# Layer 1's value products taken two steps in a row, first transfers in another order, last product in two pieces

## The chip, the cores and the metric
The kernel runs on one core of a Trainium2 chip. The metric is the device time of one execution in microseconds, as the median of several runs. The engines are named as in the profile: PE is TensorE (matrix products; PEld are its weight loads), DVE is VectorE, ACT is ScalarE, POOL is GpSimd, and SP (SyncE) issues the transfers (DMA). PSUM is the memory into which TensorE writes its products.

## The reference
Two layers run over 512 latent and 256 context tokens with D = 1024. Six modulation rows come from the conditioning vectors (adaLN). Layer 0 mixes tokens by windowed attention with 2 key/value heads and a sink, layer 1 by differential attention; behind each stands a squared-ReLU MLP of width 4096. Only the latent tokens are returned, so layer 1's context tokens serve as keys and values alone.
```python
mod_x = jax.nn.silu(c) @ w_ada[i] + b_ada[i]
hx = x * (1.0 + sc1) + sh1
# layer 1, in each of 8 heads
s = jnp.einsum('bqhtd,bkhtd->bhtqk', qblk, keys) * scale
p = jax.nn.softmax(s, axis=-1)
a = p[:, :, 0] - lam * p[:, :, 1]
o = jnp.einsum('bhqk,bkhe->bqhe', a, v_all)
o32 = o32 * lax.rsqrt(jnp.mean(jnp.square(o32), axis=-1, keepdims=True) + SUBLN_EPS)
# both layers
x = layer_norm(alpha * x + g1 * ax, ln1_g[i], ln1_b[i])
fx = sqrelu_mlp(x * (1.0 + sc2) + sh2, mlp_w1[i], mlp_w2[i])
x = layer_norm(alpha * x + g2 * fx, ln2_g[i], ln2_b[i])
```

## The kernel before
All data are fp32. A weight or activation is split into a high part that TensorE takes (fp32r) and the low rest, and a product is three matmuls (`mm3`, lines 322 to 324: high times high, then each low part times the other's high). `wsplit` loads a weight tile of 128x1024, ACT casts its high part (w_h, line 264), DVE subtracts to get the low part (w_l, line 312).

TensorE's order is written by a planner: `Flow` runs generators (projections, scores, attention, MLP) against a model of the engines' times and picks at each step who issues next; what it picks is fixed when the program is built. The other engines follow the order in which the generators emit. Output tiles in PSUM come from two sets of slots, 2 of 1024 columns for the scores (s_ps) and 4 of 512 columns for all else, so a tile can begin when the engine that reads the former one is done.

**Start.** `load_const` loads small constants, `dma` all larger tiles, all from SP's one queue. cT, badaT (bias of the modulation), ident (the identity for transposes) and lnT (layer norm parameters) are the first four; then `start_load(0)` issues four w_ada tiles, the first two tiles of the transposed x, the first key/value weight (a_wkv) and the first query weight. TensorE multiplies w_ada (ada_ps, line 364), ACT copies the rows (ada_rows), TensorE transposes them (ada_t, line 388, with ident), and DVE makes the modulation (mods) of them. hx = x times scale plus shift is then made by ACT (high part) and by DVE and POOL (low part), and the key/value products (kv_ps) follow, k-block by k-block. `setup` loads further constants later.

**Layer 1's attention** runs over 8 heads. `proj1` projects one 128-token block tb at a time (qkv_ps, 24 matmuls, issued in sixes; 384 columns for the four latent blocks, tb 0 to 3, and 256 for the two context blocks), `post1` makes rope (DVE, POOL), splits v (vt), k (sk) and q (sq), and transposes the last two (kT_ps line 1251, qT_ps line 1266). `scores1` forms the scores (s_ps, line 1347) for a 128-query block; DVE takes the negative maximum (nm), ACT the exponential, DVE the difference of the two maps (rc, nl, e). `att1` transposes e (pT_ps, line 1413), splits it (pT), and multiplies with v: one value step `av` is six matmuls of 128x256 into o_ps (line 1385). A head has six transposes and six value steps, and in each pass through its loop `att1` takes either a transpose (if `room()`) or one value step. After two heads each (0 and 1, 2 and 3, 4 and 5, 6 and 7) the norm over the head is made: rms_ps (line 1444), rmsT (1458), rr on POOL, rmsB (1473), rh and rl, rms_bc (1483, 1485), oraw. While this goes on the next head's context keys (sk, kT_ps) and projections run, and DVE splits the next head's weights (w_l of 768 columns).

**The end.** `tok_product` forms the second MLP product (y_ps, 512 columns, 24 matmuls for each token block and half). Behind the last one DVE multiplies by the gate (g_tmp, line 563), adds to acc, takes the statistics (bn), normalises, and SP sends acc out (line 1566).
```python
yield lambda: YES if room() or (pend and fl.ok(pend[0][3])) else NO
if room():
```


## Time and profile before

| what | value |
|---|---|
| median of 3 runs (lowest to highest) | 1686.93 us (1686.22 to 1688.71) |
| the profiled execution | 1690.51 us, span 1688.7 us, mean granted clock 0.991 |
| busy, share of the span | PE 96%, PEld 82%, DVE 57%, ACT 39%, POOL 20% |
| chain that ended last | PE 74%, DVE 10%, issue 5%, ACT 4%, DMA 3%, POOL 3% |

The profiled execution's time is the device time; the span is that from the first to the last instruction in its trace. Busy shares are means over the whole span. The chain is followed back from the last instruction to whatever released it each time. The granted clock is TensorE's, as a share of 2.4 GHz: 0.5 is 1.2 GHz. In rows of a timeline the first number is the start in us, the second the length; neighbouring rows of one group are merged (x4); in square brackets stands the idle time of the engine ahead of it and what ended it.

### The profile page before, as it was taken

To read this page: it belongs to the slowest core of one execution; us is meant where nothing else is said; L and a number is where in the kernel's file an instruction comes from. 1 tells how busy PE (TensorE), PEld (TensorE's weight loads), DVE (VectorE), ACT (ScalarE), POOL (GpSimd) and SP (SyncE) were. 2 spreads that over 40 slices of the span, in tenths; PEclk is the share of its full clock that TensorE was granted. 3 is DMA by queue.
4 is the path that set the end of the run, shared out by engine and by line. 5 is a ranking of instruction groups with operands and counts; after the bars stand their busy time and mean duration, and the time that the engine had idled before them with its cause. 6 is when DMAs were issued, how large, how long until landed. Compare 5 with 4: busy or idle time off the path is not lost.

```text
span 1688.7 us, 23443 instructions
## 1 busy us (share of the span) xinstructions
PE 1617.0 (96%) x9129; PEld 1392.0 (82%) x9129; DVE 956.7 (57%) x1811; ACT 658.2 (39%) x1281; POOL 344.4 (20%) x314
## 2 busy tenths in 40 slices
PE   6899999999999999999999999999989899999997
PEld 4787677789889889979978998999877788888886
DVE  3665787567756344344446777677656552332436
ACT  3454565362223113202316555555543533222230
POOL 1243544100001101243220223221101001103422
PEclk9999999999999999999999999999999899999999
DMA  9111451434445334234313122211133323132321
GB/s 365 42 51 37 170 175 35 136 125 130 145 138 162 100 125 150 100 113 139 109 59 110 51 69 67 69 45 38 47 113 111 102 80 120 63 125 75 112 88 50
DMA packets 57239, 174.77 MB, mean 103 GB/s; under 512 B 7144, under 2 KB 13096, under 8 KB 57128
## 3 DMA queue, kind: packets, MB, share of 16 engines
q1 hardware_dynamic: 57128, 173.27, 30.6%
q8 instruction: 72, 1.18, 0.3%
q14 instruction: 39, 0.32, 0.1%
HBM read 165.35 MB, written 7.90 MB: 103 GB/s over the span
## 4 chain that ended last, share of the span: by engine, by line
PE 74%; DVE 10%; issue 5%; ACT 4%; DMA 3%; POOL 3%; SPq 0%; POOLq 0%; DVEq 0%; ACTq 0%
PE y_ps L324 10%; PE y_ps L323 10%; PE y_ps L322 10%; PE h_ps L322 8%; PE h_ps L323 8%; PE h_ps L324 8%; PE o_ps L1031 2%; PE qkv_ps L322 2%; PE qkv_ps L323 2%; PE s_ps L1347 2%; PE qkv_ps L324 2%; DVE w_l L312 2%; PE pT_ps L1049 2%; DVE e L260 1%; PE o_ps L1385 1%
## 5 line engine op out<-in xcount | busy, mean ns | idle before, releaser
L264 ACT CAST w_h<-w_raw 128x1024 fp32r<-128x1024 f32 (+1 forms) x185 | 186.4, 1014 | 413.1 <-PE y_ps L324 208.6
L312 DVE TENSOR_TENSOR w_l<-w_raw,w_h 128x1024 fp32r<-128x1024 f32 (+1 forms) x185 | 220.9, 1205 | 220.6 <-ACT w_h L264 219.7
L323 PE MATMUL y_ps<-w_l,hid 128*128 128x512 f32 x640 | 252.9, 395 | 1.8 <-DVE w_l L312 1.7
L324 PE MATMUL y_ps<-w_h,hid 128*128 128x512 f32 x640 | 252.9, 395 | 0.7 <-DVE hid L260 0.7
L322 PE MATMUL y_ps<-w_h,hid 128*128 128x512 f32 x640 | 253.1, 395 | 0.0
L268 POOL TENSOR_TENSOR relu<-relu 128x768 f32<-128x768 f32 (+1 forms) x48 | 80.4, 1674 | 608.2 <-ACT relu L264 608.2
L324 PE MATMUL h_ps<-hx0m,w_l 128*128 128x384 f32 (+1 forms) x528 | 175.7, 333 | 1.6 <-DVE w_l L312 1.6
L322 PE MATMUL h_ps<-hx0m,w_h 128*128 128x384 f32 (+1 forms) x528 | 175.7, 333 | 0.2 <-ACT w_h L264 0.2
L323 PE MATMUL h_ps<-hx0m,w_h 128*128 128x384 f32 (+1 forms) x528 | 175.3, 332 | 0.0
L323 PEld LDWEIGHTS y_ps<-w_l,hid 128*128 128x128 f32 x640 | 120.4, 188 | 31.1 <-DVE w_l L312 3.3
L324 PEld LDWEIGHTS y_ps<-w_h,hid 128*128 128x128 f32 x640 | 120.4, 188 | 30.1 <-DVE hid L260 2.0
L322 PEld LDWEIGHTS y_ps<-w_h,hid 128*128 128x128 f32 x640 | 120.4, 188 | 28.7 <-ACT hid L264 0.4
L322 PE MATMUL qkv_ps<-w_h,hx 128*128 128x384 f32 (+1 forms) x384 | 127.8, 333 | 0.1
L323 PE MATMUL qkv_ps<-w_l,hx 128*128 128x384 f32 (+1 forms) x384 | 123.2, 321 | 0.3 <-DVE w_l L312 0.2
L324 PE MATMUL qkv_ps<-w_h,hx 128*128 128x384 f32 (+1 forms) x384 | 123.0, 320 | 0.0
L268 POOL TENSOR_TENSOR e<-e,sm 128x512 f32<-128x512 f32 (+2 forms) x96 | 94.1, 995 | 115.4 <-DVE sm L260 76.9
L322 PE MATMUL h_ps<-hx1m,w_h 128*128 128x512 f32 (+1 forms) x288 | 107.7, 374 | 3.6 <-ACT relu L264 3.6
L323 PE MATMUL h_ps<-hx1m,w_h 128*128 128x512 f32 (+1 forms) x288 | 107.3, 372 | 0.0
L324 PE MATMUL h_ps<-hx1m,w_l 128*128 128x512 f32 (+1 forms) x288 | 107.2, 372 | 0.0
L324 PEld LDWEIGHTS h_ps<-hx0m,w_l 128*128 128x128 f32 x528 | 99.1, 188 | 2.9 <-DVE w_l L312 2.9
L322 PEld LDWEIGHTS h_ps<-hx0m,w_h 128*128 128x128 f32 x528 | 99.1, 188 | 0.8 <-ACT w_h L264 0.6
L323 PEld LDWEIGHTS h_ps<-hx0m,w_h 128*128 128x128 f32 x528 | 99.1, 188 | 0.1
(225 smaller groups left out, 3112.6 us busy)
## 6 DMA issues: line engine op xcount, KB each, us to landing
w_raw<-in_w SPq DMA_DIRECT2D x128, 512.0 KB, 3.5
w_raw<-in_w_adaT SPq DMA_DIRECT2D x56, 512.0 KB, 3.5
w_raw<-in_w_ada SPq DMA_DIRECT2D x24, 512.0 KB, 4.0
w_raw<-in_b_w SPq DMA_DIRECT2D x32, 384.0 KB, 3.6
raw<-in_w_ada SPq DMA_DIRECT2D x16, 512.0 KB, 9.6
w_raw<-in_a_wq SPq DMA_DIRECT2D x8, 512.0 KB, 4.7
w_raw<-in_a_wo SPq DMA_DIRECT2D x8, 512.0 KB, 3.4
w_raw<-in_b_wo SPq DMA_DIRECT2D x8, 512.0 KB, 3.5
```

Of the source, the lines that this page charges most:

```text
L260: fn(**kw)
L264: fn(**kw)
L268: fn(**kw)
L312: last["split"] = nc.vector.tensor_tensor(**kw)
L322: nc.tensor.matmul(out=o, lhsT=lh, rhs=rh, start=start, stop=False)
L323: nc.tensor.matmul(out=o, lhsT=lh, rhs=rl, start=False, stop=False)
L324: last["pe"] = nc.tensor.matmul(out=o, lhsT=ll, rhs=rh, start=False, stop=stop)
L1031: nc.tensor.matmul(out=po[odd * HD:odd * HD + HD, 0:256], lhsT=vv[:, kb, kvh], rhs=pt_[:, odd * 256:odd * 256 + 256], start=(i == 0), stop ...
L1049: nc.tensor.transpose(out=pp[:, c * P:(c + 1) * P], in_=es[j][:, i * P:(i + 1) * P], identity=ident)
L1347: nc.tensor.matmul(out=sp[:, c * 512:c * 512 + 384], lhsT=qTt[:, tt, hl, qb * P:(qb + 1) * P], rhs=kS[:, tt, c * 384:c * 384 + 384], start ...
L1385: nc.tensor.matmul(out=po[:, qp * 256:(qp + 1) * 256], lhsT=vt[:, kb, vl], rhs=pt_[:, pl, a * 256:a * 256 + 256], start=(kp == 0 and pl == ...
```

## The change
Three places change. At the start badaT, ident and lnT leave the head of SP's queue: ident and badaT are issued after the first four w_ada tiles, lnT in `setup`, and a_wkv stands ahead of the two xT tiles. In `att1` a value step is taken only when two are ready (or the last ones, or when no pT buffer is free), and then both are issued in a row. In the last token block's last half of layer 1's MLP the product is formed in two pieces of 256 columns, each with its own g_tmp and add.
```diff
@@ -587,7 +587,7 @@
 
 
     def tok_product(pool, src, W, seq, acc, gates, done=None, st=None, scale=1.0, extra=None, pre={}, sink=None,
-                    late=(1,)):
+                    late=(1,), fine=False):
         st = st or {}
         Ws = {}
         if not callable(W):
@@ -601,6 +601,32 @@
                 yield sm_.ok
                 pt, u0 = psm("y_ps"), 0
                 give = lambda x, i=sm_.take(): sm_.give(i, x)
+            if fine and i == len(seq) - 1:
+
+                for c in range(2):
+                    if c:
+                        yield sm_.ok
+                        pt = psm("y_ps")
+                        give = lambda x, i=sm_.take(): sm_.give(i, x)
+                    cs_ = slice(half * 512 + c * 256, half * 512 + c * 256 + 256)
+                    tok = slice(tb * P, (tb + 1) * P)
+                    for u in range(4):
+                        w = Ws[half][u]
+                        yield w.t
+                        for k in (2 * u, 2 * u + 1):
+                            c_ = slice((k % 2) * 512 + c * 256, (k % 2) * 512 + c * 256 + 256)
+                            mm3(pt[:, 0:256], hxs(src, k, 0, tok), hxs(src, k, 1, tok), w.h[:, c_], w.l[:, c_], k == 0,
+                                k == KT - 1)
+                        p = fl.pe(6 * mm(256))
+                        if c:
+                            fl.finish(w.rel)
+                    tm = pool.tile([P, 256], F32, name="g_tmp", tag="tmp", bufs=2)
+                    m = dv(256, [p], nc.vector.tensor_tensor, out=tm, in0=pt[:, 0:256], in1=gates[0][:, cs_], op=ALU.mult)
+                    give(m)
+                    r = dv(256, [m], nc.vector.tensor_tensor, out=acc[tb][:, cs_], in0=acc[tb][:, cs_], in1=tm, op=ALU.add)
+                st[tb], r = stats(acc[tb], half, r, st.get(tb))
+                done(tb, st[tb], r)
+                continue
             left = {u for h, b in seq[i + 1:] if h == half for u in range(pre[(h, b)][2] if (h, b) in pre else 0, 4)}
             for u in range(u0, 4):
                 w = Ws[half][u]
@@ -730,13 +756,14 @@
                 gates = yield from row_gates()
             yield from tok_product(pool, hid, lambda half: [wsplit(t["w2"][l, ch, half, u]) for u in range(4)],
                                    [(h_, tb) for h_ in range(2) for tb in range(ntb)], acc, gates,
-                                   done if ch == 3 else None, extra=extra, sink=sum_up(ch, gates) if ch < 3 else None)
+                                   done if ch == 3 else None, extra=extra, sink=sum_up(ch, gates) if ch < 3 else None,
+                                   fine=l == 1 and ch == 3)
 
 
     l0 = ExitStack()
     apool = l0.enter_context(tc.tile_pool(name="apool0", bufs=4, reuse_waits="tile"))
     adap.append(l0.enter_context(tc.tile_pool(name="adap", bufs=1)))
-    badaT = load_const("badaT", [P, DEPTH, 6, KT], adap[0])
+    badaT = adap[0].tile([P, DEPTH, 6, KT], F32, name="c_badaT")
     hx = hx_tiles(apool, "hx0")
     st1 = {}
     y_spill = dram.tile([NTB, P, 512], F32, name="y_spill")
@@ -748,7 +775,6 @@
         cs = pool.tile([P, KT, 32], F32, name="cs", tag="cs")
         nc.vector.memset(cs, 0.0)
         nc.vector.tensor_copy(out=cs[:, :, 0:2], in_=sig)
-        nc.vector.tensor_copy(out=identr, in_=load_const("ident", [P, P], pool))
 
 
         def qtile(i, name, dt=F32R):
@@ -768,13 +794,15 @@
 
         def start_load(g):
             Wa = [ada_load(t["w_ada"][0, m, g, u], next(raws)) for m in (1, 0) for u in range(2)]
+            if g == 0:
+                nc.vector.tensor_copy(out=identr, in_=load_const("ident", [P, P], pool))
+                nc.sync.dma_start(out=badaT, in_=t["badaT"])
+                Wkv.append(wsplit(t["a_wkv"][0]))
             xs = []
             for k in (2 * g, 2 * g + 1):
                 x, gr, rr = next(raws)
                 x = x[:, 0:TOK]
                 xs.append((k, x, dma(TOK, [gr], out=x, in_=t["xT"][:, k]), rr))
-            if g == 0:
-                Wkv.append(wsplit(t["a_wkv"][0]))
             if g == 2:
                 hl = [pool.tile([P, 1024], F32R, name="w_kv", tag="x4", bufs=3) for _ in range(2)]
                 Wkv.append(wsplit(t["a_wkv"][1], hl=hl + [None, None]))
@@ -855,8 +883,9 @@
             nc.sync.dma_start(out=nsink, in_=t["a_sink"].broadcast_to([P, A_HEADS]))
             scale_inplace(nsink, -1.0)
             nc.sync.dma_start(out=mask, in_=t["mask"])
-
-        lnT = load_const("lnT", [P, DEPTH, 4, KT])
+            nc.sync.dma_start(out=lnT, in_=t["lnT"])
+
+        lnT = const.tile([P, DEPTH, 4, KT], F32, name="c_lnT")
         nsink = const.tile([P, A_HEADS], F32, name="nsink")
         mask = pool.tile([P, 6, P], F32, name="mask", tag="mask")
 
@@ -1397,8 +1426,11 @@
                 def room():
                     qp = i // 3
                     return i < 6 and len(ers) > qp * 2 + 1 and fl.ok([sm_.ok, xS1.ok, ers[qp * 2], ers[qp * 2 + 1]])
-                yield lambda: YES if room() or (pend and fl.ok(pend[0][3])) else NO
-                if room():
+
+                def ready_():
+                    return pend and (len(pend) > 1 or i == 6 or not fl.ok(xS1.ok)) and fl.ok([x[3] for x in pend[:2]])
+                yield lambda: YES if room() or ready_() else NO
+                if len(pend) < 2 and room() or not ready_():
                     if po is None:
                         yield sm_.spare
                         po = psm("o_ps")
@@ -1423,7 +1455,8 @@
                     pend.append((kp, qp, pt_, r, xi))
                     i += 1
                 else:
-                    p = av(*pend.pop(0))
+                    for _ in range(min(2, len(pend))):
+                        p = av(*pend.pop(0))
             st["att"] = hd_
 
 
```
**DVE at the start**, from the second group of mods to the first w_l (raw becomes x times scale plus shift, and from it hx's low part is made). Before:
```order
L260 TENSOR_TENSOR mods_81<-ada_red,c_badaT 128x4
L260 TENSOR_SCALAR raw_127<-raw_127,mods_81 128x512
L260 TENSOR_SCALAR raw_127<-raw_127,mods_81 128x256
L260 TENSOR_TENSOR hx_91<-raw_127,hx_91 128x512
L260 TENSOR_SCALAR raw_129<-raw_129,mods_81 128x512
L260 TENSOR_SCALAR raw_129<-raw_129,mods_81 128x256
L260 TENSOR_TENSOR hx_91<-raw_129,hx_91 128x512
L312 TENSOR_TENSOR w_l<-w_raw,w_h 128x1024 x2
```

After the change:
```order
L260 TENSOR_TENSOR mods_81<-ada_red,c_badaT 128x4
L312 TENSOR_TENSOR w_l<-w_raw,w_h 128x1024
L260 TENSOR_SCALAR raw_132<-raw_132,mods_81 128x512
L260 TENSOR_SCALAR raw_132<-raw_132,mods_81 128x256
L260 TENSOR_TENSOR hx_90<-raw_132,hx_90 128x512
L260 TENSOR_SCALAR raw_134<-raw_134,mods_81 128x512
L260 TENSOR_SCALAR raw_134<-raw_134,mods_81 128x256
L260 TENSOR_TENSOR hx_90<-raw_134,hx_90 128x512
L312 TENSOR_TENSOR w_l<-w_raw,w_h 128x1024
```

The first w_l (of a_wkv) now stands ahead of the six multiply-adds and subtractions, the second (of a_wq) stays behind them.

**PE at the passage from head 1 to head 2**, from rmsB to the first scores of head 2; of the qkv_ps matmuls of 128x384, which repeat in threes, one three is shown. Before, where twelve of them stand ahead of kT_ps and six behind it:
```order
L1473 MATMUL rmsB<-identr,rr 2x128 x4
L322 MATMUL qkv_ps<-w_h,hx_7757 128x384
L323 MATMUL qkv_ps<-w_l,hx_7757 128x384
L324 MATMUL qkv_ps<-w_h,hx_7757 128x384
L1251 MATMUL kT_ps<-identr,sk 128x128 x2
L1483 MATMUL rms_bc<-rh,id_8248 128x512
L1485 MATMUL rms_bc<-rl,id_8248 128x512
L1347 MATMUL s_ps<-kS_8975,qT_8976 128x384 x8
```

After the change, where six stand, behind kT_ps:
```order
L1506 MATMUL rmsB<-identr,rr 2x128 x4
L1280 MATMUL kT_ps<-identr,sk 128x128 x2
L322 MATMUL qkv_ps<-w_h,hx_7757 128x384
L323 MATMUL qkv_ps<-w_l,hx_7757 128x384
L324 MATMUL qkv_ps<-w_h,hx_7757 128x384
L1516 MATMUL rms_bc<-rh,id_8248 128x512
L1518 MATMUL rms_bc<-rl,id_8248 128x512
L1376 MATMUL s_ps<-kS_8975,qT_8976 128x384 x8
```

kT_ps (the last context block's keys) moved up to directly behind rmsB, past twelve projections. DVE's rows in this passage have a vt more ahead of three w_l and rl, which stand ahead of sk as before; after the change the passages from heads 1, 3 and 5 read alike on PE and DVE, as that from head 5 does before.

**PE in the middle of head 1**, from the last score tile to the projections behind it (the row of three qkv_ps is again shown once). Before, where 24 qkv_ps follow, six of tb 2 and 18 of tb 3:
```order
L1413 MATMUL pT_ps<-identr,e_9059 128x128
L1385 MATMUL o_ps<-pT,vt_8449 128x256 x6
L1347 MATMUL s_ps<-kS_8447,qT_8448 128x384 x4
L1385 MATMUL o_ps<-pT,vt_8449 128x256 x6
L1251 MATMUL kT_ps<-identr,sk 128x128 x2
L1385 MATMUL o_ps<-pT,vt_8449 128x256 x6
L1266 MATMUL qT_ps<-identr,sq 128x128 x4
L322 MATMUL qkv_ps<-w_h,hx_7757 128x384
```

After the change, where the last six of tb 2's qkv_ps stand ahead of s_ps, and 12 of tb 3 follow qT_ps:
```order
L1445 MATMUL pT_ps<-identr,e_9059 128x128
L322 MATMUL qkv_ps<-w_h,hx_7757 128x384
L323 MATMUL qkv_ps<-w_l,hx_7757 128x384
L324 MATMUL qkv_ps<-w_h,hx_7757 128x384
L1376 MATMUL s_ps<-kS_8447,qT_8448 128x384 x4
L1414 MATMUL o_ps<-pT,vt_8449 128x256 x12
L1280 MATMUL kT_ps<-identr,sk 128x128 x2
L1295 MATMUL qT_ps<-identr,sq 128x128 x4
```

The end of tb 2's projection moved ahead of the last score tile, two value steps stand in one row, and kT_ps and qT_ps stand together.

**DVE at the same place**; rope and vt are those of tb 2. Before:
```order
L260 SCALAR_TENSOR_TENSOR e_9095<-e_9148,nl,e_9095 128x768
L260 TENSOR_TENSOR pT<-pT_ps,pT 128x512
L260 TENSOR_REDUCE nm<-s_ps 128x1
L260 SCALAR_TENSOR_TENSOR ep<-s_0_8270 128x8
L260 RECIPROCAL rc<-sm 128x1
L260 SCALAR_TENSOR_TENSOR nl<-s_0_8270,nlam,rc 128x1
L260 SCALAR_TENSOR_TENSOR e_9186<-e_9215,nl,e_9186 128x768
L260 TENSOR_TENSOR vt_8977<-qkv_ps,vt_8977 128x128
L260 TENSOR_TENSOR rope_9258<-qkv_ps,c_cosT 128x256
L260 TENSOR_TENSOR rope_9259<-qkv_ps,c_sinT 128x4x32 x2
```

After the change:
```order
L260 SCALAR_TENSOR_TENSOR e_9095<-e_9148,nl,e_9095 128x768
L260 TENSOR_TENSOR pT<-pT_ps,pT 128x512
L260 TENSOR_REDUCE nm<-s_ps 128x1
L260 TENSOR_TENSOR vt_8977<-qkv_ps,vt_8977 128x128
L260 TENSOR_TENSOR rope_9252<-qkv_ps,c_cosT 128x256
L260 TENSOR_TENSOR rope_9253<-qkv_ps,c_sinT 128x4x32 x2
L260 RECIPROCAL rc<-sm 128x1
L260 SCALAR_TENSOR_TENSOR ep<-s_0_8270 128x8
L260 SCALAR_TENSOR_TENSOR nl<-s_0_8270,nlam,rc 128x1
L260 SCALAR_TENSOR_TENSOR e_9186<-e_9215,nl,e_9186 128x768
```

vt and rope moved from behind the second e to directly behind the last nm.

## Rows read from the trace of the kernel before
**Rows 1.** Waits of TensorE, 946 to 1282 us (in total, times, longest)
```profile
PE kT_ps L1251 <- DVE sk L260: 7.1, 5, 2.3
...
PE pT_ps L1413 <- DVE pT L260: 1.2, 2, 0.8
```

**Rows 2.** Timeline of TensorE, start (start, us, what; idle ahead)
```profile
9.75 0.69 PE L388 MATMUL ada_t<-identr,ada_rows 128*128 128x128 f32 x2 [0.49 <-ACT ada_rows L264]
...
17.41 0.58 PE L322 MATMUL kv_ps<-w_h,hx 128*128 128x256 f32 x1 [3.93 <-ACT w_h L264]
...
20.16 0.41 PE L324 MATMUL kv_ps<-w_h,hx 128*128 128x256 f32 x1
```

**Rows 3.** Timeline of ScalarE, start
```profile
12.37 0.37 ACT L264 COPY ada_rows<-ada_ps 128x256 f32<-128x256 f32 x1 [2.67 <-PE ada_ps L364]
...
16.33 1.98 ACT L264 CAST w_h<-w_raw 128x1024 fp32r<-128x1024 f32 x2
```

**Rows 4.** Timeline of SyncE's issues, start
```profile
1.19 0.42 SPq L283 DMA_DIRECT2D c_badaT<-in_badaT  x1
...
2.60 1.85 SPq L275 DMA_DIRECT2D raw<-in_w_ada  x4
```

**Rows 5.** Chain in order of time, 0 to 21 us (start, us)
```profile
4.50 7.37 DMA raw<-in_xT
```

**Rows 6.** DMA issues, 0 to 45 us (KB each, us to landing)
```profile
c_cosT<-in_cosT SPq DMA_DIRECT2D x1, 128.0 KB, 8.3
...
c_ident<-in_ident SPq DMA_DIRECT2D x1, 64.0 KB, 1.9
```

**Rows 7.** Timeline of the vector engine, start
```profile
14.77 0.91 DVE L260 TENSOR_SCALAR raw<-raw,mods 128x512 f32<-128x512 f32 x2 [0.88 <-ACT hx L264]
...
19.66 1.21 DVE L312 TENSOR_TENSOR w_l<-w_raw,w_h 128x1024 fp32r<-128x1024 f32 x1
```

**Rows 8.** Timeline of all engines, end
```profile
1679.61 0.39 PE L323 MATMUL y_ps<-w_l,hid 128*128 128x512 f32 x1
...
1679.84 0.40 PE L324 MATMUL y_ps<-w_h,hid 128*128 128x512 f32 x1
...
1680.28 0.69 DVE L563 TENSOR_TENSOR g_tmp<-y_ps,g2x 128x512 f32<-128x512 f32 x1
```

**Rows 9.** Timeline of TensorE, end of head 6
```profile
1229.35 0.28 PE L323 MATMUL qkv_ps<-w_l,hx 128*128 128x256 f32 x1
1229.47 0.28 PE L324 MATMUL qkv_ps<-w_h,hx 128*128 128x256 f32 x1
1231.19 0.33 PE L1251 MATMUL kT_ps<-identr,sk 128*128 128x128 f32 x2 [1.44 <-DVE sk L260]
```

**Rows 10.** Timeline of the vector engine, head 1
```profile
1004.75 0.95 DVE L260 TENSOR_REDUCE nm<-s_ps 128x1 f32<-128x768 f32 x1
...
1008.34 0.42 DVE L260 TENSOR_TENSOR rope<-qkv_ps,c_cosT 128x256 f32<-128x256 f32 x1
```

**Rows 11.** Timeline of TensorE, head 2
```profile
1053.90 0.37 PE L1251 MATMUL kT_ps<-identr,sk 128*128 128x128 f32 x2 [1.70 <-DVE sk L260]
```

**Rows 12.** Windows: length, busy us per engine, PEclk, DMA share, GB/s
```profile
1018.72:1030.03 11.31, 10.29 (x72) 9.05 (x72) 6.65 (x13) 5.47 (x12) 2.40 (x2) 1.00 0.53 166
...
1184.94:1198.14 13.20, 10.87 (x66) 9.21 (x66) 8.35 (x15) 6.42 (x14) 1.65 (x1) 0.84 0.45 150
1054.00:1057.40 3.40, 3.40 (x14) 3.30 (x15) 0.82 (x4) 0.76 (x3) 1.46 (x2) 0.51 0.12 41
1194.00:1200.80 6.80, 6.80 (x21) 6.03 (x20) 4.59 (x7) 2.87 (x5) 0.00 (x0) 0.50 0.28 99
```

**Rows 13.** Timeline of TensorE, head 1
```profile
1004.01 1.37 PE L1385 MATMUL o_ps<-pT,vt 128*128 128x256 f32 x6
...
1005.51 0.41 PE L322 MATMUL qkv_ps<-w_h,hx 128*128 128x384 f32 x1
```

**Rows 14.** Timeline of the vector engine, head 5 to 6
```profile
1188.00 2.70 DVE L312 TENSOR_TENSOR w_l<-w_raw,w_h 128x768 fp32r<-128x768 f32 x3 [0.47 <-ACT w_h L264]
```

## The prediction
> **What bounds the kernel now.** The page comes first: TensorE is busy for 96% of the span, so time is to be had only where TensorE stands still or runs at its lower clock. Its waits by cause come next: in layer 1's attention (946.3 to 1281 us) the largest is kT_ps behind the vector engine's sk, 7.1 us in 5 times [rows 1]. Then three places are read instruction by instruction, one for each part of the change: the first 21 us, the attention, the last 9 us. What lies between is one TensorE stream in unchanged order, so a gain or loss ahead of it shifts it whole and counts in full at the end.
>
> **Part A, the start.** After the two adaLN transposes TensorE waits 3.93 us for w_h of the first key/value weight, runs one product, and goes on without gaps only from 20.16 [rows 2], when w_l (begun 17.99, behind the two k-blocks' hx work) is there. ScalarE casts w_h at 16.33, behind four hx activations [rows 3], though the load could have been there sooner.
>
> Transfers first. Four constants stand ahead of the w_ada loads; badaT was issued at 1.19, the first w_ada at 2.60 [rows 4]. With badaT, ident and lnT gone from there, the four w_ada loads go out 1.41 us earlier. The first xT (384 KB) landed at 4.50+7.37 = 11.87 [rows 5]; taking its share off at the queue's 0.4 MB/us, the last w_ada landed near 10.8, and now at 9.4. ident (64 KB) took 1.9 us on an empty queue, cosT (128 KB) 8.3 us behind larger loads [rows 6]; I take the second kind of landing, ident at about 9.6, its cast at 9.85, so the first transpose stands at 9.9 instead of 9.75 [rows 2]: a loss of 0.15 on the chain to mods. The other end: ident lands before the last w_ada and the chain gains up to 1.4.
>
> Then the weight. wkv follows ident and badaT directly: 11.87 - 1.41 + (128+112) KB at 0.4 = about 11.05. ScalarE has the second ada_rows until 12.74 [rows 3], so w_h runs 12.75 to 13.75; the vector engine has the mods until about 13.9, w_l alone takes 1.21 [rows 7], so 15.1; the first block's two multiply-adds and the subtraction then take 0.9 and 0.7 [rows 7, 8], so hx's low part is ready near 16.75, and the dense stream begins there instead of 20.16: 3.4 gained. POOL's hx stays under it. What is late next: the third key/value group, whose hx follows ada_t number two. Ahead of it now stand one q group and eight ada matmuls (about 2.4 us) where two q groups and eight did (about 4); the chain to hx takes about 3.1 (0.5 for mods, 0.8 for ScalarE, 1.6 on the vector engine, and the hand-overs), so 0.7 comes back. **Start: -2.7, bounds -1.4 (only the queue's shift comes through) and -4.1.**
>
> **Part C, the end.** The last product's 24 matmuls of 512 columns become 48 of 256. Start to start a 512 takes 0.23, a 256 0.12 [rows 8, 9]: 24 x (0.24 - 0.23), with the scatter about 0.1 lost. The last g_tmp and acc add, 0.70 each from start to start at 512 columns [rows 8], become 256 wide, 0.42 by rope's row of that width [rows 10]; the first piece's lie under the second's 2.9 us of matmuls. **End: 0.1 - 0.56 = -0.45**, bounds -0.3 and -0.6. The Trainium skill ("TensorE: Matmul & The Clock Gate", section "Back-to-back issue gap") gives 518 cycles for 512 columns and 262 for 256; by it the loss would be 24 x 6 cycles, an estimate of 0.06, and the end -0.5. The spacings here are longer than either figure.
>
> **Part B, the attention.** Two value steps in a row (12 o_ps) make the planner's order alike in all odd and in all even heads. There are three effects.
>
> *Even heads.* In head 2 kT_ps waits 1.70 for sk [rows 11]; right after it TensorE runs 3.4 us at 1.2 GHz [rows 12], which costs half, 1.7; the third pT then waits 0.8 [rows 1], and s_ps 0.5 for ScalarE's e. Head 6's kT_ps waits 1.44 [rows 9]. In the new order 18 matmuls of 256 columns (2.1 us) stand between the projections and that kT, and sk has its time. I count all of it as gone: -4.7 and -1.4, and -0.5 for the small waits of head 4. The two s_ps waits over 1 us stand in head 7, which loses nothing. Sum -6.6.
>
> *Odd heads and head 0.* Ahead of the last latent block's projection (tb 3) now stand 12 o_ps, kT and qT; before, the end of tb 2's projection and tb 3's stood in one row. tb 3's first matmul writes the PSUM slot that tb 2's rope has to free, and this rope is now on the vector engine behind the reduction nm of the eighth score tile. Head 1: TensorE came to that point at 1005.51 after a wait of 0.49 inside o_ps [rows 13]; with the wait gone, and six matmuls of 384 columns (6 x 0.174) in the place of a value step (6 x 0.12), it comes near 1005.25. The vector engine starts nm at 1004.75 (0.95), then vt, and rope of 0.42 and twice 0.24 [rows 10]: free at 1006.6. A new wait of 1.35, against 0.49 + 0.34 that vanish: with rounding +0.55. By the same reading +0.4, +0.55, +0.4 in heads 0, 3, 5. Sum +1.9. Behind it are queued only TensorE's own matmuls; the chain to the last e waits for ScalarE at that point anyway, and its transposes, at 1008.7, come 0.5 after it. Bounds: 0 if the slot comes from another tile, +4 if none of the old waits go.
>
> *The passages from heads 1, 3, 5 to the next.* From the rms product to the last of eight s_ps, the first passage took 11.31 and the third 13.20 [rows 12]. The third is the one where kT stands right behind rmsB, and kT there waits 2.3 [rows 1]: three w_l of 0.9 [rows 14] and rl stand ahead of its sk on the vector engine. After the change all three passages have this order, on TensorE and on the vector engine word for word. Worked out: the third has six matmuls of 256 more and twelve of 384 less than the first, 1.38 less work, and its last 4.1 us (1194.0 to 1198.14) run at half clock, which costs up to 2.05, taken as 1.8 since TensorE waits a little there anyhow, so its order costs 13.20 - 1.8 + 1.38 - 11.31 = +1.45. Twice: +2.9.
>
> *The clock there.* Behind the third passage's wait the granted clock is 1.2 GHz for 6.8 us [rows 12], up to half of it lost; less those little waits I take 3.05. Does it fall in the two new places too? What TensorE does before is the same; I take a fall as in head 2, 3.4 us, at both: 1.6 each, between 0 and 3.05. +3.2.
>
> **Attention: -6.6 + 1.9 + 2.9 + 3.2 = +1.4**, bounds -2 (no fall of the clock) and +5.
>
> **Sum: -2.7 - 0.45 + 1.4 = -1.75.** The profiled execution took 1690.51, 3.6 above the median of the three runs; the sum holds for it (1688.8) and is carried over to the median, 1686.93 - 1.75 = **1685.2 us**.
>
> **The rivals.** A difference under 0.2% (3.4 us) can't be told from none.
> 1. *The clock holds at both passages* (2.4 GHz throughout): -1.75 - 3.2 = -4.9, 1682.0, faster. For it: head 6's wait of 1.44 left the clock up [rows 9]; against: the third passage's longer one didn't.
> 2. *Both passages lose the whole 3.05*: +2.9, net +1.15, 1688.1, no difference. For it: the order is the third passage's.
> 3. *Slower*: the new waits of 1.1 to 1.4 in heads 0, 1, 3 and 5 each pull the clock down as head 2's 1.70 did. 1.7 each, +6.8, net +5.0, 1691.9. It decides from four such falls on (three give +3.3, no difference). Against: head 6 again.
> 4. *The start doesn't do what it should*: the weight is there early, but the hx chain behind late mods still sets the stream, and only 1.4 comes through. Net -0.45, 1686.5, no difference.
> 5. *ident lands as quickly as on the empty queue*, 1.9 us after its issue: then mods come up to 1.4 sooner, the start is -4.1, net -3.15, 1683.8, no difference. cosT's 8.3 [rows 6] speaks against it. The Trainium skill ("DMA: Bandwidth & Descriptors", section "Queues, rings and completion order") says that completion isn't first-in, first-out, so that a later transfer may finish ahead of an earlier one; by that rule this rival is the case, and no row of this trace shows such an overtaking.
>
> **How the numbers follow.** Forecast 0.42; rivals 0.25, 0.15, 0.08, 0.06, 0.04. The forecast's own spread (start -1.4 to -4.1, odd heads 0 to 4) puts a quarter of it beyond -3.4: 0.1, and rival 5 lends 0.01; with rival 1, whose own spread leaves a tenth inside, faster is 0.34 in all. Slower is rival 3 and a little of rival 2: 0.09. The rest is 0.57. The range goes from rival 1 with the start's upper end, 1682.0 - 1.4 = 1680.6, to rival 2 with the start's lower end, 1688.1 + 1.3, taken as 1689.2.
>
> **What would show it.** Right: the first L324 on kv_ps near 16.8, with a wait under 1 us before the third key/value group; the rmsB wait for POOL gone in both passages and two more kT_ps waits of about 2.3, each with a PEclk near 0.5 behind it; new waits of about 1.3 for rope ahead of qkv_ps in heads 0, 1, 3, 5; no kT wait in heads 2 and 6; last y_ps to span end shorter by about 0.55. Wrong: ada_t's first transpose before 9 or after 11; kT after rmsB without a wait; a low clock anywhere else in the attention; or a load that lands late between 21 and 60 us, where TensorE had next to no wait before.

## The result and the profile after

The changed kernel is slower: median 1695.6 us (1689.36 to 1696.47, 7 runs) against 1688.71 us (1686.22 to 1691.33, 7 runs) of the kernel before on the same chip, a ratio of 1.0038 [1.0026, 1.005] (in brackets the 95% interval, here and below). The prediction said 1685.2, within 1680.6 to 1689.2; time and direction were both missed. The profiled execution took 1696.4 us, 5.9 more than the one of before, with a span of 1694.5 us. Six of the seven runs have a mean granted clock of 0.986 or 0.987 and lie between 1694.7 and 1696.5; the seventh has 0.991 and took 1689.36.

The page of the changed kernel: the span, the busy time of each engine with its share and instructions, and the granted clock in 40 slices.
```profile
span 1694.5 us, 23501 instructions
PE 1623.0 (96%) x9153; PEld 1397.9 (82%) x9153; DVE 959.6 (57%) x1813; ACT 658.0 (39%) x1281; POOL 346.5 (20%) x314
...
PEclk9999999999999999999999999999899899999999
```

TensorE's busy share is what it was. Two slices of the clock's row stand at 8, the 29th and the 32nd (1186 to 1229 and 1313 to 1356 us); shorter falls don't show in slices of 42 us, and the windows below are needed. Half speed stood here, before and after (start and length in us, from the clock's records in the trace; the last column adds up what lies between 946 and 1282 us):

| | stretches at 1.2 GHz | in the attention |
|---|---|---|
| before | 313.4 (3.4), 1054.1 (3.4), 1194.0 (6.8), 1252.0 (3.4), 1310.1 (10.2), 1685.5 (5.2) | 13.6 |
| after | 310.0 (3.4), 1023.4 (6.8), 1112.1 (6.8), 1197.4 (10.2), 1258.9 (3.4), 1316.9 (6.8), 1347.6 (3.4), 1689.0 (7.7) | 27.2 |

The waits of TensorE by cause, whole span of the changed kernel (the answer to [rows 1] and to the start's waits): engine, tile and line <- releaser: us in total, times, longest.
```profile
PE kT_ps L1280 <- DVE sk L260: 9.4, 6, 2.3
...
PE ada_ps L364 <- DMA raw<-in_w_ada: 5.3, 1, 5.3
PE pT_ps L1445 <- DVE e L260: 4.5, 5, 1.9
...
PE qkv_ps L322 <- DVE rope L260: 3.8, 4, 1.3
...
PE ada_t L388 <- DVE identr L798: 2.1, 1, 2.1
```
rope's wait is new, e's was 1.9 in one piece, kT_ps has grown from 7.9 to 9.4, rmsB's 2.1 for POOL and the 3.93 us for w_h at the start are gone.

The start, TensorE of the changed kernel (answers to [rows 2]).
```profile
5.30 2.28 PE L364 MATMUL ada_ps<-raw,cs 128*32 128x256 f32 x16 [5.30 <-DMA raw<-in_w_ada]
9.66 0.66 PE L388 MATMUL ada_t<-identr,ada_rows 128*128 128x128 f32 x2 [2.07 <-DVE identr L798]
...
14.67 0.58 PE L322 MATMUL kv_ps<-w_h,hx 128*128 128x256 f32 x1 [1.31 <-ACT hx L264]
...
16.35 0.58 PE L324 MATMUL kv_ps<-w_h,hx 128*128 128x256 f32 x1 [0.80 <-DVE hx L260]
```
The dense stream begins at 16.35 instead of 20.16.

The passage from head 1, TensorE of the changed kernel (it answers to the third passage before, in [rows 1] and [rows 12]); ahead of it the wait in head 1 (against [rows 13]), behind it one in head 2 (against [rows 11]), and last the kT_ps of the two other passages.
```profile
1001.68 0.41 PE L322 MATMUL qkv_ps<-w_h,hx 128*128 128x384 f32 x1 [1.34 <-DVE rope L260]
...
1018.40 0.60 PE L1506 MATMUL rmsB<-identr,rr 128*2 128x128 f32 x4
1021.32 0.37 PE L1280 MATMUL kT_ps<-identr,sk 128*128 128x128 f32 x2 [2.32 <-DVE sk L260]
...
1024.22 2.93 PE L1376 MATMUL s_ps<-kS,qT 128*128 128x384 f32 x8
...
1050.82 0.98 PE L1445 MATMUL pT_ps<-identr,e 128*128 128x128 f32 x7 [1.11 <-DVE e L260]
...
1111.41 0.36 PE L1280 MATMUL kT_ps<-identr,sk 128*128 128x128 f32 x2 [2.33 <-DVE sk L260]
...
1197.69 0.49 PE L1280 MATMUL kT_ps<-identr,sk 128*128 128x128 f32 x2 [2.33 <-DVE sk L260]
```
The eight s_ps behind the wait take 2.93 us, where eight at full clock take 1.68 (in the fourth experiment's rows below). The vector engine meanwhile (as [rows 14] of the third passage before):
```profile
1017.05 2.70 DVE L312 TENSOR_TENSOR w_l<-w_raw,w_h 128x768 fp32r<-128x768 f32 x3 [0.47 <-ACT w_h L264]
1019.71 0.68 DVE L260 TENSOR_TENSOR rl<-rmsB,rh 2x512 fp32r<-2x512 f32 x1
1020.32 0.27 DVE L260 TENSOR_TENSOR vt<-qkv_ps,vt 128x128 fp32r<-128x128 f32 x1
1020.97 0.29 DVE L260 TENSOR_TENSOR sk<-qkv_ps,sk 128x128 fp32r<-128x128 f32 x1 [0.39 <-ACT sk L264]
```
The windows of the three passages of the changed kernel, ahead of the fall and in it: stretch, its length, busy us of each engine (with instructions), granted clock, DMA share, GB/s.
```profile
1004.09:1023.40 19.31, 16.78 (x134) 15.38 (x133) 9.87 (x21) 9.82 (x22) 6.29 (x7) 1.00 0.36 110
1023.40:1030.20 6.80, 6.80 (x22) 6.15 (x21) 4.53 (x6) 3.22 (x6) 0.00 (x0) 0.50 0.22 60
1104.09:1112.10 8.01, 5.68 (x50) 5.07 (x51) 4.86 (x10) 4.78 (x11) 1.66 (x1) 1.00 0.37 110
1112.10:1118.90 6.80, 6.80 (x20) 5.52 (x19) 4.31 (x6) 2.45 (x6) 0.00 (x0) 0.50 0.36 116
1190.37:1197.40 7.03, 4.99 (x46) 4.38 (x45) 4.62 (x10) 4.04 (x9) 1.65 (x1) 1.00 0.27 87
1197.40:1207.60 10.20, 9.91 (x29) 8.63 (x30) 5.72 (x8) 4.03 (x7) 0.00 (x0) 0.50 0.36 135
```
In each, TensorE waited 2.3 us for sk (until 1021.32, 1111.41 and 1197.69). The granted clock went to 0.50 at 1023.4, 1112.1 and 1197.4, from 0.2 us ahead of the wait's end to 2.1 behind it, and stayed there for 6.8, 6.8 and 10.2 us in which TensorE hardly stood still.

The end, vector engine of the changed kernel (answers to [rows 8]).
```profile
1686.81 0.42 DVE L260 TENSOR_TENSOR g_tmp<-y_ps,g2x 128x256 f32<-128x256 f32 x1
1687.26 0.42 DVE L260 TENSOR_TENSOR acc<-acc,g_tmp 128x256 f32<-128x256 f32 x1
...
1688.76 1.40 DVE L260 SCALAR_TENSOR_TENSOR acc<-acc,mv,l2g 128x512 f32<-128x512 f32 x2
```
From the last g_tmp to the first normalising instruction it is 1.95 us; before it was 2.49 (from 1680.28).

**Where the time went.** A head's norm is counted from its rms_ps, which is formed behind every head (rmsT and what follows it behind every second one). How far the same instruction stands later than before (minus: sooner): -2.8 us at 60 us, -5.5 at 906, -5.3 at head 0's norm, -4.7, -3.2, -0.8, +4.0, +5.4, +6.2 and +8.6 at those of heads 1 to 7 (2.8 of the last is y_ps work that now stands ahead of it), +5.8 at the end. The stretches between the heads' norms, as elapsed time less the number of matmuls in them times their spacing at full clock (the excess, in us), and what the prediction's terms make of each (head 0's +0.4 lies ahead of the first):

| from norm to norm | excess before | excess after | change | forecast |
|---|---|---|---|---|
| 0 to 1 | 3.0 | 3.6 | +0.6 | +0.55 |
| 1 to 2 | 8.0 | 8.9 | +0.9 | -1.65 |
| 2 to 3 | 2.5 | 5.5 | +3.0 | +0.55 |
| 3 to 4 | 3.3 | 8.1 | +4.8 | +2.55 |
| 4 to 5 | 1.8 | 2.6 | +0.8 | +0.4 |
| 5 to 6 | 9.1 | 9.5 | +0.4 | -1.4 |
| 6 to 7 | 9.0 | 8.9 | -0.1 | 0 |

So part C did what was forecast, part A at 60 us as well, and part B took +10.3 in these stretches where it was to take about +1. The further 2.7 us between 60 and 906 us are not shown to be part A's: the profiles of the second and the ninth experiment, which keep the start of before, stand 2.4 and 1.0 us sooner over the same stretch than the profile of before.

### The profile page after: what moved, and what is told of

It is laid out like the page before. It is cut to its first block, busy times and chain, and to the rows that moved or that the text cites. A ratio compares the mean times of both kernels' runs of the same rounds, so it can differ in the third digit from the quotient of the medians.

```text
span 1694.5 us, 23501 instructions
## 1 busy us (share of the span) xinstructions
PE 1623.0 (96%) x9153; PEld 1397.9 (82%) x9153; DVE 959.6 (57%) x1813; ACT 658.0 (39%) x1281; POOL 346.5 (20%) x314
## 4 chain that ended last, share of the span: by engine, by line
PE 76%; DVE 10%; ACT 4%; issue 4%; DMA 3%; POOL 2%; SPq 0%; DVEq 0%; POOLq 0%; ACTq 0%
PE y_ps L324 10%; PE y_ps L323 10%; PE y_ps L322 10%; PE h_ps L322 8%; PE h_ps L323 8%; PE h_ps L324 8%; PE qkv_ps L322 3%; PE qkv_ps L323 3%; PE qkv_ps L324 2%; PE o_ps L1060 2%; PE s_ps L1376 2%; DVE w_l L312 2%; PE pT_ps L1078 2%; DVE e L260 1%; PE o_ps L1414 1%
## 5 line engine op out<-in xcount | busy, mean ns | idle before, releaser
L323 PE MATMUL y_ps<-w_l,hid 128*128 128x512 f32 (+1 forms) x648 | 254.3, 392 | 1.8 <-DVE w_l L312 1.7
L324 PE MATMUL y_ps<-w_h,hid 128*128 128x512 f32 (+1 forms) x648 | 254.3, 392 | 0.5 <-DVE hid L260 0.3
L322 PE MATMUL y_ps<-w_h,hid 128*128 128x512 f32 (+1 forms) x648 | 254.5, 393 | 0.3 <-ACT hid L264 0.3
```

Source lines behind the costliest of these rows:

```text
L322: nc.tensor.matmul(out=o, lhsT=lh, rhs=rh, start=start, stop=False)
L323: nc.tensor.matmul(out=o, lhsT=lh, rhs=rl, start=False, stop=False)
L324: last["pe"] = nc.tensor.matmul(out=o, lhsT=ll, rhs=rh, start=False, stop=stop)
```

## The experiments

**My theory** after the result: TensorE's order with pairs is the one foreseen, waits too, and what was mis-sized is the clock. Behind each of the three waits of 2.3 us for sk TensorE works at half speed for 6.8 to 10.2 us. **The rival**: the waits themselves (2.3 three times, rope's 1.3, e's 1.1) and the changed order explain the loss, and the clock follows from how often TensorE stands still in all, whatever one does in one place. Comparisons are ratios to the kernel before, run on the same chip beside each (four kernels to a chip). Diffs are against the changed kernel unless another is named.

**1. Start and end alone** (value steps single as before).
```diff
-                if len(pend) < 2 and room() or not ready_():
+                if room():
...
-                    for _ in range(min(2, len(pend))):
-                        p = av(*pend.pop(0))
+                    p = av(*pend.pop(0))
```


> The changed kernel with the value steps taken singly as before (only the start and the end changed). Theory 1 (the attention's new order costs what the change lost): the start's 2.8 us, what layer 0 adds to it, and the end's 0.5 come through: 3 to 6 us below the kernel before, ratio 0.9965 to 0.998, and the two early passages keep their clock. Rival (what the start gains is given back before the attention): within 1 us of the kernel before.

Measured 1683.37 us, ratio 0.998 [0.9969, 0.9991]: 3.9 us less than before, near what the start and the end were to give together (3.15). Its own profile stands 1.2 us sooner at 60 us and 4.1 at 906, so single profiles split this gain differently. The passage from head 5 has the order and the wait that it had before. TensorE's rows there, and the window behind them:
```profile
1184.10 0.60 PE L1502 MATMUL rmsB<-identr,rr 128*2 128x128 f32 x4
1187.02 0.37 PE L1280 MATMUL kT_ps<-identr,sk 128*128 128x128 f32 x2 [2.32 <-DVE sk L260]
```
```profile
1187.00:1200.00 13.00, 12.98 (x73) 12.23 (x74) 10.67 (x19) 6.94 (x16) 0.74 (x1) 1.00 0.31 98
```
Here the clock held. The same wait in the same place is followed by a fall in one profile and not in another.

**2. Pairs alone** (the kernel before with part B).

> The kernel before with nothing but the paired value steps. Theory 1: 8 to 11 us above the kernel before, ratio 1.005 to 1.0065, with kT_ps waits of 2.3 us and 1.2 GHz behind all three passages. Rival (the clock falls because of the earlier start, which shifts all that follows): at most 4 us above, with full clock behind the first two passages.

Measured 1700.29 us, ratio 1.0083 [1.0068, 1.0097], more than expected: 13 us lost. Half speed behind the three passages lasted 10.2, 6.8 and 10.2 us. Parts A and C together are worth 0.45% beside the pairs and 0.2% alone; the longer falls here go with that, what made them longer was not traced.

**3. The vector engine's w_l behind sk.** In the passages three of the four w_l wait until sk of the last block is out (the fourth stood behind it already); TensorE's order is the changed kernel's, row for row.
```diff
+            if after:
+                tc.add_manual_dep(last["split"].ins, after, ORDER, reason="later")
...
-                yield lambda: YES if st["att"] >= hd_ - 2 else NO
+                yield lambda: YES if st["att"] >= hd_ - 2 and st.get("last", -1) >= hd_ - 1 else NO
+                late_ = lambda u: st["sk"] if hd_ in (3, 5, 7) and u else None
...
-                W = st2["W"] if hd_ == 0 else [wsplit(t["b_w"][hd_, u], 768) for u in range(4)]
+                W = st2["W"] if hd_ == 0 else [wsplit(t["b_w"][hd_, u], 768, after=late_(u)) for u in range(4)]
```


> The changed kernel, in which the vector engine splits the second and third weight of heads 3, 5 and 7 behind the sk of the passage; TensorE's order is the same row for row. Theory 1 (the wait of kT_ps brings the clock down): the waits of 2.3 us shrink to under 1, the clock stays at 2.4 GHz in at least two of the three passages, 8 to 13 us below the changed kernel, that is 1 to 6 us below the kernel before. Rival (the clock falls whatever the wait is): only the waits go, 3 to 5 us below the changed kernel, 1.2 GHz still behind the passages.

Measured 1684.72 us, ratio 0.9992 [0.9978, 1.0006]. Its vector engine in the first passage:
```profile
1020.89 0.27 DVE L260 TENSOR_TENSOR sk<-qkv_ps,sk 128x128 fp32r<-128x128 f32 x1
1021.09 2.67 DVE L312 TENSOR_TENSOR w_l<-w_raw,w_h 128x768 fp32r<-128x768 f32 x3
```
The wait of kT_ps fell from 2.3 to 1.6 us, 2 us in all three together; the ratio fell by 0.46%, 7.8 us. The rest is the clock's: in its attention only one stretch (1110.3, 3.4 us) is at half speed. Its runs scatter from 1680.2 (clock 0.995) to 1694.2 (0.987), so the shorter wait seems to save the clock in most runs and not in all (one has a profile, of the others only the mean clock is known).

**4. The wait filled.** Eighteen matmuls of 256 columns into the unread half of kT_ps's own tile, ahead of kT_ps for the last block of heads 2, 4 and 6. They add work and compute nothing.
```diff
+            for _ in range(18 if tb == NTB - 1 and hd_ in (2, 4, 6) else 0):
+                nc.tensor.matmul(out=pk[:, 256:512], lhsT=identr, rhs=hxs(hx, 0, 0, slice(0, 256)), start=True, stop=True)
```


> The changed kernel, in which 18 more matmuls of 256 columns (2.1 us, into the half of the kT_ps tile that nobody reads) stand ahead of kT_ps in each of the three passages: the wait for sk is as long as before but TensorE works through it. Theory 1 (idleness brings the clock down): 2.4 GHz through the passages, 6 to 10 us below the changed kernel. Rival (the clock isn't the cost): no more than 1 us from the changed kernel, or slower.

Measured 1684.37 us, ratio 0.9984 [0.9975, 0.9994]. TensorE in its first passage, and the windows behind the three:
```profile
1016.12 0.60 PE L1508 MATMUL rmsB<-identr,rr 128*2 128x128 f32 x4
1016.47 2.35 PE L1280 MATMUL kT_ps<-hx,identr 128*128 128x256 f32 x18
1019.04 0.37 PE L1282 MATMUL kT_ps<-identr,sk 128*128 128x128 f32 x2 [0.22 <-DVE sk L260]
...
1021.58 1.68 PE L1378 MATMUL s_ps<-kS,qT 128*128 128x384 f32 x8
```
```profile
1023.00:1030.00 7.00, 7.00 (x42) 7.00 (x41) 5.92 (x13) 3.42 (x8) 0.58 (x1) 1.00 0.02 6
1112.00:1119.00 7.00, 7.00 (x43) 6.97 (x43) 5.88 (x15) 4.24 (x11) 0.73 (x1) 1.00 0.01 2
1192.00:1202.00 10.00, 10.00 (x60) 9.96 (x59) 8.92 (x18) 5.97 (x14) 0.74 (x1) 1.00 0.10 39
```
From rmsB to kT_ps it is 2.92 us, as in the changed kernel (1018.40 to 1021.32): kT_ps comes not one tenth sooner, TensorE is only kept at work. The clock holds through all three passages, and with 54 matmuls more the kernel is 0.54% faster than the changed one, 9 us. In the two profiles the stretches between the norms that hold the three passages are 3.1, 3.0 and 4.5 us shorter, behind which the changed kernel had 6.8, 6.8 and 10.2 us of half speed. That is the clock's share of the loss, and it decides against the rival.

**5. Pairs in even heads alone** (parts A and C kept).
```diff
+                pair = hd_ % 2 == 0
...
+                    if not pair:
+                        return pend and fl.ok(pend[0][3])
...
-                    for _ in range(min(2, len(pend))):
+                    for _ in range(min(2 if pair else 1, len(pend))):
```


> The changed kernel with paired value steps in heads 2, 4 and 6 (and 0) alone; odd heads take them singly as before, and so the passages from heads 1 and 3 keep the order of the kernel before. Theory 1 (the pairs pay in even heads, and what they lose they lose in odd heads and in the passages behind these): heads 2 and 6 lose their kT_ps waits of 1.7 and 1.4 us and the clock's fall, 2 to 5 us below the run with start and end alone, that is 6 to 9 us below the kernel before. Rival (an order with pairs brings waits of its own wherever it is used): no more than 1 us below start and end alone.

Measured 1679.34 us, ratio 0.9953 [0.9941, 0.9965]: 0.27% under the first experiment, 4.6 us. In even heads the pairs do bring a good part of what was forecast for them (6.6): its kT_ps waits are 3.7 us in 2 pieces where the first experiment has 7.1 in 5.

**6. The same with w_l behind sk** in the one passage (into head 6) that still has the wait.

> As the run with pairs in even heads alone, and in the passage from head 5 the vector engine splits the second and third weight of head 7 behind sk. Theory 1: the last passage's wait shrinks from 2.3 to 1.6 us and the clock holds there; 0.7 to 4 us below pairs in even heads alone. Rival: the wait doesn't matter, same time.

Measured 1676.82 us, ratio 0.9943 [0.9929, 0.9958], not to be told from the fifth. Its profile has half speed for 6.8 us from 1187.1, behind a wait of 1.6: a shorter wait doesn't always save the clock.

**7. tb 2's rope ahead of nm** (on the third): the vector engine does it first in heads 0, 1, 3 and 5.

> The changed kernel with w_l behind sk in the passages, and besides tb 2's rope emitted ahead of the last nm in heads 0, 1, 3 and 5 (its job comes ahead of the scores), which also moves the planner's order around it. Theory 1: the four waits of 1.3 us for rope ahead of qkv_ps go, 2 to 5 us below w_l behind sk. Rival (the wait goes elsewhere, into pT or kT): within 1 us of w_l behind sk.

Measured 1689.31 us, ratio 1.0005 [0.9996, 1.0014]; not faster than the third kernel, its basis (0.9992), and by the intervals not shown to be slower. Its waits in the attention:
```profile
PE kT_ps L1285 <- DVE sk L260: 8.7, 6, 1.7
PE qkv_ps L325 <- DVE w_l L312: 3.8, 3, 1.3
PE pT_ps L1453 <- DVE e L260: 2.9, 2, 1.9
...
PE qkv_ps L324 <- DVE rope L260: 0.9, 2, 0.5
```
rope's 3.8 became 0.9, and w_l's and sk's took its place. It is not a clean test of rope's wait, since the planner moved the passages' order as well; in this order what rope's wait gave back, the others took.

**8. Third and fourth together** (10 fillers each).

> The changed kernel with w_l behind sk, and ten matmuls of 256 columns (1.2 us, into the unread half of the kT_ps tile) ahead of kT_ps in the three passages, in the 1.6 us that are still waited there. Theory 1 (only idleness matters): the clock stays at 2.4 GHz in all three passages, 1 to 3 us below the filled wait alone. Rival (the passages are no longer where the clock is lost): the same as w_l behind sk.

Measured 1683.24 us, ratio 0.9971 [0.996, 0.9983]; no half speed in the passages. Between this and the third kernel lies 0.2%, between this and the fourth 0.13%, and the intervals overlap: most of the gain is had by either remedy.

**9. The kernel before with fillers** (18, ahead of head 6's kT_ps alone).

> The kernel before, with 18 matmuls of 256 columns (2.1 us, into the unread half of the kT_ps tile) ahead of kT_ps in its one passage with the 2.3 us wait, from head 5 to head 6; nothing else. Theory 1 (the idle wait brings the clock down): 2.4 GHz behind that passage, 2 to 4 us below the kernel before. Rival (the filled runs gained by something else): within 1 us of the kernel before.

Measured 1684.99 us, ratio 0.998 [0.9969, 0.9991]. The kernel before, too, gets 0.2% (3.4 us) faster by 18 matmuls that compute nothing in its one passage of this kind; the excess from head 5 to 6 falls from 9.1 to 4.0 us. The window behind it holds its clock:
```profile
1192.00:1202.00 10.00, 10.00 (x56) 9.54 (x56) 8.25 (x16) 4.60 (x11) 0.74 (x1) 1.00 0.27 93
```

**10. Pairs in odd heads alone** (as the fifth, with `hd_ % 2 == 1`).

> The changed kernel with paired value steps in heads 1, 3, 5 and 7 alone. Theory 1 (the loss is the odd heads' and their passages'): 9 to 14 us above the run with start and end alone, that is 5 to 10 us above the kernel before, with the 2.3 us wait in all three passages and the rope waits of 1.3 us. Rival (only pairs in all heads together make the loss): under 3 us above start and end alone.

Measured 1697.09 us, ratio 1.0053 [1.0037, 1.0068], 0.73% (12 us) over the first experiment: all of the loss comes with the pairs in odd heads. Its largest wait in the attention, and two of its windows at half speed:
```profile
PE kT_ps L1280 <- DVE sk L260: 12.9, 8, 2.3
PE qkv_ps L322 <- DVE rope L260: 3.6, 3, 1.3
```
```profile
1023.90:1030.70 6.80, 6.80 (x20) 5.52 (x19) 4.47 (x7) 2.23 (x4) 0.00 (x0) 0.50 0.27 91
1201.40:1208.20 6.80, 6.80 (x21) 6.05 (x20) 4.53 (x6) 3.01 (x5) 0.00 (x0) 0.50 0.40 131
```
The two halves add up: +0.73% and -0.27% on 0.998 make 1.0026, and the changed kernel has 1.0038 [1.0026, 1.005].

**11. Even pairs, w_l behind sk, and 10 fillers in head 6.**

> Pairs in even heads alone, w_l behind sk in the last passage, and ten matmuls of 256 columns in the 1.6 us that kT_ps still waits there. Theory 1: the clock holds at that passage, 1 to 3 us below the run without the ten, 10 to 13 us below the kernel before. Rival: the same as without them.

Measured 1677.85 us, ratio 0.9937 [0.9921, 0.9953]; its profile has no half speed in the passage. In the median it can't be told from the sixth. The sixth's runs fall into two groups (1675.2 to 1677.6, and 1682.0 and 1682.3, its profile among the latter), these lie between 1674.9 and 1679.1 without the upper one; six runs each are too few to call that shown.

**12. The eleventh with ident ahead of the four w_ada loads.**
```diff
+            idt = load_const("ident", [P, P], pool) if g == 0 else None
...
-                nc.vector.tensor_copy(out=identr, in_=load_const("ident", [P, P], pool))
+                nc.vector.tensor_copy(out=identr, in_=idt)
```


> As the run before this one, but ident is issued ahead of the four first w_ada loads instead of behind them (64 KB, one issue). If ident's place behind the loads delays the first transpose (the prediction's 9.9): the first ada_t stands 1 us or more sooner, and the dense kv_ps stream up to 1 us sooner. Rival (the a_wkv cast and w_l set the stream, or the w_ada loads come that much later): the stream starts within 0.3 us of where it did, same time.

Measured 1677.97 us, ratio 0.9938 [0.9918, 0.9958], the same as the eleventh. The start did move:
```profile
8.65 0.69 PE L390 MATMUL ada_t<-identr,ada_rows 128*128 128x128 f32 x2 [0.49 <-ACT ada_rows L264]
...
15.52 0.58 PE L326 MATMUL kv_ps<-w_h,hx 128*128 128x256 f32 x1 [0.80 <-DVE hx L260]
```
ada_t stands 1 us sooner and the stream begins at 15.52. One microsecond is too little for this measurement, all the more as this profile shows half speed at 1188.1 for 3.4 us despite the fillers.

The tally of the passages over all profiles: behind an unfilled wait of 2.3 us the clock fell in 11 of 12 (three in the changed kernel, three in the second experiment, three in the tenth, one in the fifth, one before; it held in the first), behind one of 1.6 us in 2 of 4 (third and sixth), behind a filled one in 1 of 9. Taken over all of TensorE's waits of 1.4 us or more for kT_ps in layer 1's attention, in all 14 profiles, with falls that begin within 3 us of the wait's end: 11 of 12 behind 2.3 us, 5 of 11 behind 1.6 to 1.75, 1 of 20 behind 1.4 to 1.5.

## Why the prediction was wrong, point by point

- **Start, -2.7: right**, but the match to a tenth is luck. It is -2.8 at 60 us in this profile, and -1.1 to -3.0, against the same profile of before, in the ten that have this start. The stream began at 16.35 against 16.75, the first transpose at 9.66 against 9.9; of 3.8 us gained at the stream's start 0.9 came back by 33 us, near the 0.7 foreseen, though the trace lists no wait there. Rival 5 (ident overtakes) did not happen: the first two loads for the modulation were used by 7.58, the fourth landed at 9.07 and ident behind it at 9.26, and the transpose still waited for ident's cast at 9.29. The Trainium skill ("DMA: Bandwidth & Descriptors", section "Queues, rings and completion order") says that a later transfer may finish first. In this trace the small one behind four large ones did not, and ahead of them it cost 1 us less (twelfth experiment). Another 2.7 us were gained in layer 0, up to 906 us, in a stretch that the forecast called unchanged; profiles with the start of before differ there by as much as 2.4, and what made it was not traced.
- **End, -0.45: right**, -0.54.
- **Odd heads and head 0, +1.9: the mechanism was right in the odd heads**, to a hundredth in two of them (1.34 in heads 1 and 3, 0.92 in head 5, against 1.35 each), and head 0 to 1 gave +0.6 against +0.55. In head 0 there was no such wait: tb 3's first matmul began at 960.25, while tb 2's rope ran to 961.0, so it can't have waited for that slot (the prediction's bound 0); the fourth wait of the list, 0.2, stands in head 2. From head 2 to 3 and 4 to 5 it was more: in head 3 the next weight came late as well (0.56 for w_h and 0.55 for w_l, at 1071 to 1073 us), because TensorE stood 3.2 us sooner there and the load landed only 1.0 sooner (1070.68 against 1071.67).
- **Even heads, -6.6: too large.** kT_ps's waits in heads 2 and 6 are gone, as foreseen, but I counted nothing in their place. New are waits for e ahead of pT_ps (1.11 in head 2, 0.48 in each of heads 4 and 6) and 0.2 for rope. The 0.5 for head 4's small waits was too much from the start (the trace lists 0.17), and only one wait of s_ps, not two, was over 1 us (1.19, in head 7). The fifth experiment prices what is left of this term at 4.6 us.
- **The passages, +2.9: right** in order, in the wait (2.32, 2.33), in what stands ahead of sk on the vector engine, and in rmsB's waits for POOL, which are gone.
- **"The clock there", +3.2: this is the step that failed.** I read the third passage's 6.8 us at half speed, and then took "a fall as in head 2, 3.4 us", for the two new passages that had its order. They fell for 6.8 us each, and the third itself, which I had left as it was, for 10.2; with the waits filled these places came out 3.1, 3.0 and 4.5 us shorter (fourth experiment). Half of the difference is 1.7 us at each of the three, 5.1 in all, and with it the sum turns from -1.75 to +3.4; with the waits for e (2.1) and the late weight (1.1) it comes to +6.6 before layer 0's -2.7, +3.9 with it, against +5.8 in the span. So the miss of the attention was larger than the total shows, and about 2 us remain that I can't place. The profile spoke for the larger fall (the passages were word for word the third), and rival 2 had this price for two of the three; the third passage's was not in the range at all.
- **The slower rival (3)** had the wrong place: the rope waits of 1.3 us did not pull the clock down (no fall begins behind one of them in any profile).
- **How firm the size is:** the mean granted clock differs between executions of one kernel. The changed kernel's run at clock 0.991 took 6 us less than those at 0.986, and a forecast from one profile of before can't know which it will be; but that 3.4 us was the milder of two choices could have been read from the third passage alone.

By the medians the best kernels are the sixth, eleventh and twelfth, 0.57 to 0.63% under the kernel before (the fifth, 0.47% under it, can't be told from them): parts A and C, pairs where kT_ps has cover (even heads), and w_l behind sk where it hasn't.

## What to carry to other kernels

When an order rule gives a place the same order as another place in the profile, price it by that place whole, with the clock behind its wait, and not by a milder one. In this kernel, with TensorE 96% busy, a wait of 2.3 us cost 3 to 4.5 us more after it had ended (fourth experiment); so look who makes it wait and move that work behind the thing waited for, and where this can't be done, try harmless work in the gap. A rule that helps in one half of a loop and hurts in the other is to be tried on each half alone.

## What the runs showed of the hardware that was not expected

- More work, less time: 54 matmuls of 256 columns more took the changed kernel from a ratio of 1.0038 to 0.9984, and 18 took the kernel before from 1 to 0.998.
- The fall comes about at the wait's end (0.2 us ahead of it) or up to 2.7 us behind it, when TensorE is busy again (2.1 in the changed kernel's first passage, 1181.73 to 1184.4 in the fifth experiment's), and it lasts longer than the wait: 3.4, 6.8 or 10.2 us behind one and the same 2.3.
- It is not certain, and it is rarer behind shorter waits (the tally above): the 2.3 us wait in the first experiment's profile left the clock at 2.4 GHz, and the fillers in the twelfth did not keep it there.
